# A hybrid decoder block on one core: stages that take turns where they meet, quarters staged in row slots, jobs further from their rows, another product order by rows

## Chip, cores and metric

One core of a Trainium2 chip. The metric is the device time of one execution in microseconds, the median of several runs. TensorE multiplies, VectorE and ScalarE do the element-wise work, GpSimd (POOL) issues stores and takes powers, SyncE (SP) issues loads.

## What is computed

2048 tokens of width 1024, all float32, one layer:

```python
h = rms_norm(x, norm_mix)
C, B, a, u, v, gA, gB = split(h @ w_in)              # each 1024 wide
yA = B * causal_conv3(C * a)
yB = gelu(u) * (tril(W_s[head]) @ layer_norm(gelu(v)) + b)   # within chunks of 128 tokens
x = x + (sigmoid(gA) * yA + sigmoid(gB) * yB) @ w_out
hid = relu(rms_norm(x, norm_mlp) @ w_ff1) ** 2       # 4096 wide
out = rms_norm(x + hid @ w_ff2, final_norm)
```

## The kernel before

**Products.** Tokens go in two blocks of 1024. The products of in, out, ff1 and ff2 are made by a 2x2 scheme with seven products in place of eight, named "1" to "7": of the left side sums of quarters are taken (quarter sums h11, h6, h7 and so on, kept in DRAM), of the right side `weight_sums` (L303) makes them as needed. Every factor is split into a high and a low part (`split`, L128: one copy on ScalarE, one subtraction on VectorE), and `passes` (L137) multiplies three of the four pairs of parts. So each step has four groups of three matmuls of 128x512, twelve in all, recorded at L140.

**Stages.** In order: v (32 steps) and in (168) of block 0, v and in of block 1, then out 0, out 1 (28 each), ff1 0, ff1 1, ff2 0, ff2 1 (112 each). `drive` (L290) writes the program: for step s it first emits the loads of the steps up to s + 8, then the preparations (weight sums, splits) up to s + 3, then what hangs in the step's "before" list, then the step's matmuls. TensorE and SP keep this order (L1009); ScalarE, VectorE and POOL get an order made by the scheduler, in which an instruction that is ready can stand ahead of one that the source has earlier.

**By columns** (`pair_steps`, L320; in and ff1): a pair of 128-column strips of weights is one unit of seven steps in the order "1674253"; `stagger` puts neighbouring pairs into each other, so that within a stage a pair's steps alternate with another's. Only the first and last four steps of a stage stand alone. 1, 6, 7 and 4 of a pair add on to one PSUM bank, whose state after 1, 6 and 7 ScalarE copies out.

**By rows** (`row_steps`, L663; out and ff2): "1674253" again, each product over nk row strips (4 in out, 8 in each half of ff2), on four banks. After the last strip the banks are added to the rows `x1` (L715) and 6 goes on in the bank of 1. `rows_in` (L729) loads all eight rows at once.

**Buffers.** `big` has twelve slots of 4 KB a partition for rows, `rawq` nine of 2 KB for raw weights and quarters, `half` eight of 2 KB, `wunit` four prepared weight units, `hold` seven named places for prepared left sides or weight rows; PSUM has eight banks of 128x512.

**Jobs between steps.** Norm and mix jobs of the gated branch (`ln_jobs`, L456): `norm(i)` centres and scales a row on VectorE, ScalarE and POOL (L465 to L467) and splits it; `mix(i, q)` multiplies it by the chunk weights (eight matmuls at L428), and VectorE moves the result out (L484, L485). They are spread over v from step 17 and over in from step 0. Jobs for the quarters of a later stage (`quarter_jobs`, L203): `begin` loads and norms a row, `turned` transposes it (eight matmuls at L218, two banks), `sums` adds and stores quarters. `quarters` (L259) loads one later, as four 256 KB pieces into `rawq`, and splits it into its place.

## Time and profile before

| | us |
|---|---|
| median of three runs (2704.41 to 2710.7) | 2705.53 |
| the profiled execution | 2706.06 |
| its span, first to last instruction | 2704.3 |
| TensorE busy | 2578.5 (95%) |
| VectorE busy | 1923.7 (71%) |
| ScalarE busy | 1264.5 (47%) |
| GpSimd busy | 354.2 (13%) |
| mean granted TensorE clock | 0.977 |

Busy is the time in which an engine has at least one instruction under way; matmuls are pipelined, so a busy TensorE need not be at its peak, and its counts per microsecond say more. A window is a stretch of the span with start and end in us from its beginning; an instruction that overlaps an edge is counted. "Granted clock" is the share of 2.4 GHz that TensorE was allowed; 0.5 is 1.2 GHz.

### The profile page before, as it was taken

The numbers are of one execution on the slowest core, as the hardware profiler recorded it, in microseconds if no ns is written. First come the engines' busy times: TensorE is split into PE (matmuls) and PEld (weight loads), VectorE is DVE, ScalarE is ACT, GpSimd is POOL, SyncE is SP. The second block draws the span as 40 slices with busy tenths as digits, with TensorE's granted clock in tenths as the row PEclk, the third lists the DMA queues.
The fourth block names the chain that finished last, engine by engine and source line by source line (L and its number), as shares of the span: only waits on it lengthen the run. The fifth ranks groups of instructions, "written<-read, shape, count | busy, mean of one in ns | idle before, by whom it ended". The sixth has DMA issues, their size and how long they took to land. (4 is left out here: it accounts for less than half of the span.)

```text
span 2704.3 us, 33392 instructions
## 1 busy us (share of the span) xinstructions
PE 2578.5 (95%) x11405; PEld 2125.2 (79%) x11405; DVE 1923.7 (71%) x3229; ACT 1264.5 (47%) x2205; POOL 354.2 (13%) x628
## 2 busy tenths in 40 slices
PE   8899999999899999999598999999999999999998
PEld 7778887788688888887476888778887888878886
DVE  5886776675886666778676676666657768696775
ACT  6544343344544344444235555655555444554444
POOL 1230110100330000000221222211211000000001
PEclk9999999999899999999799999999999999999999
DMA  6322433426432331354776666654448363563632
GB/s 207 91 89 67 130 112 117 139 83 198 141 94 63 90 99 54 101 205 153 259 226 210 197 191 195 206 186 158 152 145 341 118 227 108 169 251 100 223 103 78
DMA packets 297392, 410.67 MB, mean 152 GB/s; under 512 B 23509, under 2 KB 188421, under 8 KB 297221
## 3 DMA queue, kind: packets, MB, share of 16 engines
q1 hardware_dynamic: 254036, 276.91, 32.4%
q0 software_dynamic: 38576, 123.24, 13.1%
q10 hardware_dynamic: 4608, 8.39, 0.8%
q8 instruction: 89, 1.46, 0.2%
q14 instruction: 83, 0.67, 0.1%
HBM read 285.24 MB, written 123.21 MB: 151 GB/s over the span
## 5 line engine op out<-in xcount | busy, mean ns | idle before, releaser
L140 PE MATMUL ps<-hold,wu 128*128 128x512 f32 x6720 | 1546.9, 392 | 30.3 <-ACT hf L126 19.6
L140 PEld LDWEIGHTS ps<-hold,wu 128*128 128x128 f32 x6720 | 1265.9, 189 | 300.4 <-ACT hf L126 25.0
L140 PE MATMUL ps<-wu,hold 128*128 128x512 f32 x4128 | 963.6, 394 | 13.1 <-DVE big L117 7.2
L140 PEld LDWEIGHTS ps<-wu,hold 128*128 128x128 f32 x4128 | 782.8, 191 | 181.4 <-ACT wu L126 5.4
L120 DVE TENSOR_TENSOR wu<-rq,wu 128x512 fp32r<-128x512 f32 x464 | 318.9, 689 | 173.2 <-ACT wu L126 171.0
L126 ACT ACTIVATE wu<-rq 128x512 fp32r<-128x512 f32 x464 | 290.3, 627 | 301.7 <-PE ps L140 167.0
L126 ACT ACTIVATE hf<-ps 128x512 f32<-128x512 f32 x240 | 143.2, 597 | 294.3 <-PE ps L140 290.6
L120 DVE TENSOR_TENSOR wu<-hf,wu 128x512 fp32r<-128x512 f32 x240 | 165.4, 689 | 160.1 <-ACT wu L126 159.4
L126 ACT ACTIVATE wu<-hf 128x512 fp32r<-128x512 f32 x240 | 150.8, 628 | 261.2 <-DVE hf L120 128.1
L120 DVE TENSOR_TENSOR hold<-rq,hold 128x512 fp32r<-128x512 f32 x368 | 238.9, 685 | 38.8 <-ACT hold L126 38.4
L126 ACT ACTIVATE hold<-rq 128x512 fp32r<-128x512 f32 x368 | 210.8, 619 | 88.8 <-DMA rq<-h2d 30.3
L126 ACT ACTIVATE wu<-hold 128x512 fp32r<-128x512 f32 x200 | 125.3, 630 | 248.7 <-PE ps L140 234.8
L120 DVE TENSOR_TENSOR wu<-hold,wu 128x512 fp32r<-128x512 f32 x200 | 137.1, 688 | 120.9 <-ACT wu L126 120.7
L783 POOL DMA_DIRECT2D hidd<-big x224 | 122.3, 546 | 458.8 <-ACT big L771 436.7
L117 DVE TENSOR_TENSOR big<-ps,hf 128x512 f32<-128x512 f32 x120 | 82.6, 688 | 59.0 <-PE ps L140 58.7
L117 DVE TENSOR_TENSOR hf<-ps,hf 128x512 f32<-128x512 f32 x96 | 66.3, 691 | 67.1 <-PE ps L140 65.8
L117 DVE TENSOR_TENSOR big<-ps,big 128x512 f32<-128x512 f32 (+1 forms) x176 | 108.2, 670 | 7.9 <-PE ps L140 6.1
L120 DVE TENSOR_TENSOR rq<-rq,rq 128x512 f32<-128x512 f32 x160 | 110.1, 688 | 3.5 <-DMA rq<-in_w_ff_dram 0.8
L819 POOL TENSOR_TENSOR st<-st,mhalf 128x1 f32<-128x1 f32 x16 | 16.1, 1009 | 611.5 <-DVE st L818 611.5
L123 DVE TENSOR_TENSOR big<-big,hf 128x512 f32<-128x512 f32 x120 | 82.6, 688 | 11.8 <-ACT hf L600 11.7
L623 POOL DMA_DIRECT2D md<-big x56 | 30.5, 546 | 456.1 <-DVE big L117 448.9
L487 POOL DMA_DIRECT2D mixd<-hf x128 | 72.4, 566 | 101.9 <-DVE hf L484 89.3
(102 smaller groups left out, 1470.7 us busy)
## 6 DMA issues: line engine op xcount, KB each, us to landing
rq<-in_w_in_dram SPq DMA_DIRECT2D x256, 256.0 KB, 3.0
hidd<-big POOLq DMA_DIRECT2D x224, 256.0 KB, 2.8
rq<-hidd SPq DMA_DIRECT2D x224, 256.0 KB, 3.8
rq<-in_w_ff_dram SPq DMA_DIRECT2D x128, 256.0 KB, 3.2
hold<-in_w_ff_dram SPq DMA_DIRECT2D x64, 512.0 KB, 7.6
big<-x1d SPq DMA_DIRECT2D x32, 512.0 KB, 8.7
md<-big POOLq DMA_DIRECT2D x56, 256.0 KB, 4.4
rq<-md SPq DMA_DIRECT2D x56, 256.0 KB, 8.0
```

The source lines that it names most:

```text
L117: nc.vector.tensor_tensor(o, a, b, ALU.add)
L120: nc.vector.tensor_tensor(o, a, b, ALU.subtract)
L123: nc.vector.tensor_tensor(o, a, b, ALU.mult)
L126: nc.scalar.activation(o, a, AF.Copy)
L140: nc.tensor.matmul(ps, lhsT=stat_of(a), rhs=mov_of(b), start=first and n == 0, stop=last and n == 2, skip_group_check=goes_on,)
L487: nc.gpsimd.dma_start(out=mixd[blk][h + e][:, c0 : c0 + P], in_=o)
L623: nc.gpsimd.dma_start(out=md[blk][p][:, j, :], in_=src)
L783: nc.gpsimd.dma_start(out=hidd[blk][p][:, i, :], in_=src)
L819: nc.gpsimd.tensor_tensor(r, v, mhalf, ALU.pow)
```

## The change

- **Turns.** A new `weave` joins the stages: the last four steps of what is there and the first four of the next stage take turns.
- **Quarters.** `quarters` loads two pieces of 512 KB into two `big` slots; it makes four splits' work in two of double width. The first stage's quarters come three steps earlier in v of block 1; for ff1 of block 0 all seven loads stand in out 1 (steps 20 to 26), for ff1 of block 1 the first two in ff1 of block 0; the preparations stay in their steps.
- **Jobs.** A norm stands four steps before its first mix (`at_mixes`: every 3 steps in v from 17, every 2 in in from 4). A row's `begin` stands eight steps before `turned` in in, six in ff1 0, and up to six in out 1, by a list of steps.
- **Row order.** "1265734". 2, 5 and 3 take banks of their own; 6, 7 and 4 go on in those of 1. P5 is added to two quarters. Rows come in two halves, at steps 1 and 6 in out (4 and 12 in ff2); in out 1 into places 5 and 3 of `hold`, not into slots. The places of weights and left sides in the row stages are others.
- **Gate.** gelu(u) * sigmoid(gB) is gathered in two `big` slots of its own; the first four quarters are written there without a multiplication. The mixed rows (`load_mix`) come two pairs later and are multiplied in at the end, in `finish`.

```diff
+ROW_ORDER = "1265734"
+ROW_QUARTERS = {
+    "1": ((0, 0),), "2": ((0, 0),), "6": ((0, 1),), "5": ((1, 1), (0, 1)),
+    "7": ((1, 1),), "3": ((0, 1),), "4": ((1, 0),),
+}
...
         def load():
-            for r in range(CH):
-                t = rq()
-                nc.sync.dma_start(out=t, in_=src[p][:, r, :])
+            for q in range(2):
+                t = slot()
+                r = src[p][:, 2 * q : 2 * q + 2, :]
+                nc.sync.dma_start(out=t.rearrange("p (r c) -> p r c", r=2), in_=r)
                 parts.append(t)
...
             def gate(act, name, last, m, n, ps, a, j=j, st=st):
+                if name == "gate" and name not in st:
+                    st[name] = [slot() for _ in range(2)]
+                    st["fresh"] = 4
+                o = st[name][n][:, tok(m)]
+                if name == "gate" and st["fresh"]:
+                    st["fresh"] -= 1
+                    nc.scalar.activation(o, plus(o, ps, a), act)
+                    return
                 t = hf()
                 nc.scalar.activation(t, plus(t, ps, a), act)
-                o = st[name][n][:, tok(m)]
                 mul(o, o, t)
...
             def finish(j, st):
                 y1, y2 = st.pop("y")
+                for g, m, y in zip(st.pop("gate"), st["mix"], (y1, y2)):
+                    mul(g, g, m)
+                    add(y, y, g)
                 m1, m2 = st.pop("mix")
-                add(y1, y1, m1)
-                add(y2, y2, m2)
...
-                if n == 2:
+                if n == 4:
                     pr["7"]["before"].append(load_mix)
...
-            first = p in "125"
-            if first and n == 0:
-                banks[GROUP[p]] = [bank() for _ in range(CH)]
+            first = p in "1253"
+            if n == 0:
+                banks[p] = [bank() for _ in range(CH)] if first else banks["1"]
...
-                m, c = {"1": (0, 0), "6": (0, 1), "7": (1, 1)}.get(p) or QUARTER[p]
-                t = x1[r + m * CH][:, c * HB : (c + 1) * HB]
-                add(t, banks[GROUP[p]][r], t)
-                if p not in "167":
-                    finish(r + m * CH, c)
+                for m, c in ROW_QUARTERS[p]:
+                    t = x1[r + m * CH][:, c * HB : (c + 1) * HB]
+                    add(t, banks[p][r], t)
+                    if p in "2734":
+                        finish(r + m * CH, c)
...
-                ("16", "72", nxt),
+                ("14", "25", nxt),
...
-        steps[2]["before"].append(lambda: rows_in(x1, lambda i: x1d[blk][i]))
+        for m in range(2):
+            steps[(4, 12)[m]]["before"].append(
+                lambda m=m: rows_in(x1, lambda i: x1d[blk][i], m)
+            )
...
+    def at_jobs(steps, n0, every, lag, jobs):
+        begin, turned, sums = jobs
+        for n in range(2 * CH):
+            i = n // 2 + CH * (n % 2)
+            s = n0 + int(n * every)
+            at(steps, s, lambda i=i: begin(i))
+            at(steps, s + lag, lambda i=i: turned(i))
+            if n % 2:
+                at(steps, s + lag + 1, lambda r=n // 2: sums(r))
...
+    def weave(steps):
+        if phases:
+            tail, head = phases[-4:], steps[:4]
+            phases[-4:] = [f for ab in zip(tail, head) for f in ab]
+            phases.extend(steps[4:])
...
-                bring(v[22 + 3 * n], *quarters(hq, h1d[blk], p))
-            bring(inn[4], *quarters(hq, h1d[blk], "3"))
-        spread(v, 17, 0.9, 16, lambda blk=blk: late[blk, 0])
-        spread(inn, 0, 0.8, 16, lambda blk=blk: late[blk, 1])
+                bring(v[19 + 3 * n], *quarters(hq, h1d[blk], p))
+            bring(inn[5], *quarters(hq, h1d[blk], "3"))
+        at_mixes(v, 17, 3, 4, lambda blk=blk: late[blk, 0])
+        at_mixes(inn, 4, 2, 4, lambda blk=blk: late[blk, 1])
...
-            spread(inn, 44, 5, len(jobs), lambda jobs=jobs: jobs)
-        phases += v + inn
+            at_jobs(inn, 44, 11, 8, jobs)
+        weave(v)
+        weave(inn)
...
-    outs = [out_steps(blk, rotate("74253")) for blk in blocks]
+    outs = [
+        out_steps(0, "16", rotate("7425"), (None, None)),
+        out_steps(1, "74", rotate("3162162"), ("5", "3")),
+    ]
...
+            load, prep = quarters(hqs[blk], h2d[blk], p)
+            s = ff1s[blk][(0, 1, 2, 3, 4, 6, 8)[n]]
+            if blk == 0:
+                at(outs[1], min(27, 20 + n), load)
+                bring(s, nothing, prep)
...
+    for n, s in enumerate((8, 9, 10, 11, 16, 17, 18, 19)):
+        i = n // 2 + CH * (n % 2)
+        at(outs[1], (2, 3, 5, 6, 10, 11, 12, 13)[n], lambda i=i: begin(i))
+        at(outs[1], s, lambda i=i: turned(i))
+        if n % 2:
+            at(outs[1], s, lambda r=n // 2: sums(r))
+    at_jobs(ff1s[0], 16, 10, 6, h2_jobs(1))
```

## Rows read from the trace of the kernel before

**Rows 1.** The page's first part: busy time, share, instructions of each engine.

```profile
PE 2578.5 (95%) x11405; PEld 2125.2 (79%) x11405; DVE 1923.7 (71%) x3229; ACT 1264.5 (47%) x2205; POOL 354.2 (13%) x628
```

**Rows 2.** Windows, L140 alone: width, PE and PEld busy (count), clock, DMA.

```profile
1800.00:1850.00 50.00, 50.00 (x223) 41.39 (x222) 1.00 0.47 153
1850.00:1900.00 50.00, 50.00 (x222) 41.42 (x221) 1.00 0.44 141
```

**Rows 3.** The same view, end of the mixes: first L140, then L428.

```profile
765.00:795.00 30.00, 26.67 (x117) 21.43 (x116) 1.00 0.38 116
...
765.00:795.00 30.00, 4.30 (x32) 4.24 (x32) 1.00 0.38 116
```

**Rows 4.** The same view, L140 alone, four stretches.

```profile
79.00:165.00 86.00, 61.57 (x248) 47.95 (x247) 0.92 0.28 83
527.00:541.00 14.00, 10.36 (x42) 8.28 (x41) 0.88 0.74 211
676.00:795.00 119.00, 90.39 (x373) 71.26 (x372) 0.93 0.42 125
1198.00:1462.00 264.00, 204.67 (x843) 163.42 (x842) 0.90 0.68 230
```

**Rows 5.** Windows, all work: width, PE, PEld, DVE, ACT, POOL busy, clock, DMA.

```profile
79.00:165.00 86.00, 74.92 (x344) 62.02 (x343) 71.28 (x179) 39.03 (x70) 29.36 (x53) 0.92 0.28 83
...
676.00:795.00 119.00, 106.28 (x501) 88.91 (x500) 98.69 (x241) 56.40 (x102) 43.48 (x75) 0.93 0.42 125
1198.00:1462.00 264.00, 213.00 (x907) 172.44 (x906) 199.33 (x328) 106.64 (x185) 38.56 (x64) 0.90 0.68 230
1740.00:1775.00 35.00, 24.70 (x93) 18.89 (x93) 26.51 (x43) 21.84 (x41) 4.89 (x9) 0.85 0.75 236
2060.00:2100.00 40.00, 35.61 (x144) 28.60 (x144) 34.99 (x59) 18.10 (x32) 3.80 (x7) 0.91 1.00 394
2374.00:2420.00 46.00, 39.71 (x162) 30.84 (x161) 40.91 (x73) 20.74 (x39) 4.49 (x4) 0.96 0.75 278
```

**Rows 6.** Waits of PE over the span: total us, times, longest.

```profile
PE ps L218 <- DVE big L201: 40.4, 8, 24.8
...
PE ps L428 <- ACT big L126: 18.8, 6, 7.4
```

**Rows 7.** The view of rows 5, in 1 to out 0.

```profile
1198.00:1225.00 27.00, 23.57 (x101) 18.30 (x100) 25.37 (x41) 14.03 (x24) 3.81 (x7) 1.00 0.86 337
```

**Rows 8.** Timeline of DVE, end of a group in in 1.

```profile
863.14 1.23 DVE L117 TENSOR_TENSOR big<-big,big 128x1024 f32<-128x1024 f32 x1
...
874.56 1.22 DVE L117 TENSOR_TENSOR big<-big,big 128x1024 f32<-128x1024 f32 x1
875.70 0.68 DVE L120 TENSOR_TENSOR hf<-rq,hf 128x512 f32<-128x512 f32 x1
876.30 0.68 DVE L117 TENSOR_TENSOR big<-big,big 128x512 f32<-128x512 f32 x1
```

**Rows 9.** Waits of SP's queue over the span: total us, times, longest.

```profile
SPq L332 <- DVE wu L120: 1129.8, 256, 12.9
```

**Rows 10.** Timeline, out 0 to out 1: start, us, what, idle before.

```profile
1289.62 2.48 DVE L117 TENSOR_TENSOR big<-ps,big 128x512 f32<-128x512 f32 x4
1290.71 2.40 POOL L748 DMA_DIRECT2D x1d<-big  x4 [12.35 <-DVE big L117]
...
1311.83 1.06 ACT L200 ACTIVATE junk<-big 128x1024 bf16<-128x1024 f32 x1 [15.31 <-DMA big<-x1d]
...
1314.65 1.97 PE L218 MATMUL ps<-ident,big 128*128 128x128 f32 x8 [24.78 <-DVE big L201]
```

**Rows 11.** DMA issues: count, KB each, median us to landing.

```profile
big<-x1d SPq DMA_DIRECT2D x32, 512.0 KB, 8.7
...
x1d<-big POOLq DMA_DIRECT2D x16, 512.0 KB, 6.1
h2d<-hf POOLq DMA_DIRECT2D x32, 256.0 KB, 5.3
```

More of the change, by code (lines that the diff above doesn't have):

```diff
@@ L250, in sums @@
                 sink("x", a21)
-        out = []
-        for r in range(CH):
-            for i in (r, r + CH):
-                out += [lambda i=i: begin(i), lambda i=i: turned(i)]
-            out.append(lambda r=r: sums(r))
-        return out
+        return begin, turned, sums
     def quarters(hq, src, p, place=None):
@@ L270, in prep @@
             t = held(place or p)
-            for r, part in enumerate(parts):
-                tr = slice(r * P, (r + 1) * P)
-                split(t[:, 0, :, tr], t[:, 1, :, tr], part.rearrange("p (k t) -> p k t", k=CH))
+            for q, part in enumerate(parts):
+                a, b = [
+                    t[:, e, :, 2 * q * P : 2 * (q + 1) * P].rearrange("p k (r t) -> p r k t", r=2)
+                    for e in range(2)
+                ]
+                split(a, b, part.rearrange("p (r k t) -> p r k t", r=2, k=CH))
             hq[p] = t
@@ L489, in mix @@
                 st.pop(i)
-        jobs = []
-        for i in range(CH):
-            jobs += [lambda i=i: norm(i), nothing, lambda i=i: mix(i, 0), lambda i=i: mix(i, 1)]
-        return jobs
+        return norm, mix
     def v_steps(blk, hq, done):
@@ L625, in u_gate @@
             def u_gate(*a, last, j=j, st=st, gate=gate):
-                gate(AF.Gelu_apprx_tanh, "mix", last, *a)
+                gate(AF.Gelu_apprx_tanh, "gate", last, *a)
             def ga_gate(*a, last, gate=gate):
@@ L631, in gb_gate @@
             def gb_gate(*a, last, gate=gate):
-                gate(AF.Sigmoid, "mix", last, *a)
+                gate(AF.Sigmoid, "gate", last, *a)
             def with_last(f, last):
@@ L702, in run @@
                 passes(
-                    banks[GROUP[p]][r],
+                    banks[p][r],
                     lambda a: h[:, a, n % CH, r * P : (r + 1) * P],
@@ L724, in row_steps, with rows_in @@
             )
-            for p in ORDER
+            for p in ROW_ORDER
             for n in range(nk)
         ]
-    def rows_in(x1, src):
-        for i in range(2 * CH):
-            x1[i] = slot()
-            nc.sync.dma_start(out=x1[i], in_=src(i))
+    def rows_in(x1, src, m, place=None):
+        t = None if place is None else held(place, F32)
+        for i in range(CH):
+            x1[m * CH + i] = slot() if t is None else t[:, i, :]
+            nc.sync.dma_start(out=x1[m * CH + i], in_=src(m * CH + i))
     def rotate(names):
@@ L836, in ff2_steps @@
                 x1,
-                ("16", "72", nxt),
+                ("14", "25", nxt),
                 finish if chunk == 1 else lambda i, h: None,
             )
-        steps[2]["before"].append(lambda: rows_in(x1, lambda i: x1d[blk][i]))
+        for m in range(2):
+            steps[(4, 12)[m]]["before"].append(
+                lambda m=m: rows_in(x1, lambda i: x1d[blk][i], m)
+            )
         return steps
@@ L917, in at, with at_mixes @@
         steps[n]["before"].append(f)
-    def spread(steps, n0, every, count, jobs_of):
-        for i in range(count):
-            at(steps, int(n0 + i * every), lambda i=i: jobs_of()[i]())
-    phases = []
+    def at_jobs(steps, n0, every, lag, jobs):
[7 more added lines that the diff above has]
+                at(steps, s + lag + 1, lambda r=n // 2: sums(r))
+    def at_mixes(steps, n0, every, lag, jobs_of):
+        for i in range(CH):
+            at(steps, n0 + i * every, lambda i=i: jobs_of()[0](i))
+            for q in range(2):
+                at(steps, n0 + i * every + lag + q, lambda i=i, q=q: jobs_of()[1](i, q))
+    phases = []
+    def weave(steps):
[3 more added lines that the diff above has]
+            phases.extend(steps[4:])
+        else:
+            phases.extend(steps)
     for blk in blocks:
@@ L939, in hybrid_block_kernel @@
                 at(v, 15 + 3 * k, lambda k=k: first_sums(k))
-            bring(inn[0], nothing, nothing)
-            at(inn, 0, first_last)
+            at(inn, 4, first_last)
         else:
@@ L966, in hybrid_block_kernel @@
         for n, p in enumerate(ORDER):
-            bring(ff1s[blk][(0, 1, 2, 3, 4, 6, 8)[n]], *quarters(hqs[blk], h2d[blk], p))
-    jobs = h2_jobs(0)
-    spread(outs[1], 1, 0.8, len(jobs), lambda jobs=jobs: jobs)
-    jobs2 = h2_jobs(1)
-    spread(ff1s[0], 16, 4, len(jobs2), lambda: jobs2)
-    for ph in outs + ff1s + [ff2_steps(blk, rotate("453")) for blk in blocks]:
-        phases += ph
+            load, prep = quarters(hqs[blk], h2d[blk], p)
[3 more added lines that the diff above has]
+                bring(s, nothing, prep)
+            elif n < 2:
+                at(ff1s[0], 7 * NPAIR - 10 + n, load)
+                bring(s, nothing, prep)
+            else:
+                bring(s, load, prep)
+    begin, turned, sums = h2_jobs(0)
+    for n, s in enumerate((8, 9, 10, 11, 16, 17, 18, 19)):
[5 more added lines that the diff above has]
+    at_jobs(ff1s[0], 16, 10, 6, h2_jobs(1))
+    for ph in outs + ff1s + [ff2_steps(blk, nxt_g) for blk in blocks]:
+        weave(ph)
     first_norm(0)
```

18 lines of the change are left out of this document (10 added, 8 removed).

## The prediction, made before the change was run

> **What bounds it now.** I read the page first: TensorE is busy 2578.5 of 2704.3 us, far ahead of VectorE (1923.7) and ScalarE (1264.5) [rows 1]. So time comes only from stretches where TensorE does less than it can. What it can: in the middle of ff1 of block 1, with no wait, 50 us hold 222 or 223 matmuls of 128x512, one at either edge counted in both windows [rows 2]. I take 222.5, that is 0.2247 us each and 2.70 us for a step of twelve. The small matmuls: in 765 to 795 TensorE is never idle at granted clock 1.00 and does 117 large ones (26.3 us) and 32 of line 428, so these cost 3.7 / 32 = 0.116 us each [rows 3]; a mix job (8 of them) is 0.93 us. I give the transposes of line 218 the same price.
>
> Next, windows around each place where two stages meet, counting large matmuls [rows 4, 5]. What is left of the width after 0.2247 us for each large and 0.116 us for each small matmul is lost:
> - A, end of v and start of in, block 0 (79 to 165): 86 - 248 x 0.2247 - 96 x 0.116 = 19.2 us.
> - B, the same in block 1 (676 to 795): 119 - 83.8 - 128 x 0.116 = 20.4.
> - C, one transpose job in in of block 0 (527 to 541): 14 - 9.4 - 0.9 = 3.7.
> - D, out 0, out 1 and the start of ff1 0 (1198 to 1462): 264 - 189.4 - 64 x 0.116 = 67.2.
> - E, ff1 0 to ff1 1 (1740 to 1775): 35 - 20.9 = 14.1.
> - F, ff1 1 to ff2 0 (2060 to 2100): 40 - 32.4 = 7.6.
> - G, ff2 0 to ff2 1 (2374 to 2420): 46 - 36.4 = 9.6.
>
> Sum 141.8 us: what the change can reach at the most. TensorE's waits name the causes [rows 6]: 40.4 us before the transposes of line 218, for a row that is not normed yet, and 18.8 us before the mixes of line 428, for the norm in front of them. The lost time is more than the gaps, as the clock drops behind them: 0.85 to 0.96 in these windows [rows 4, 5], against 1.00 in those without a wait [rows 2, 3].
>
> Then VectorE in the same windows [rows 5]: A 71.3, B 98.7, D 199.3, E 26.5, F 35.0, G 40.9 us busy, where TensorE's own work (width less loss) is 66.8, 98.6, 196.8, 20.9, 32.4, 36.4. **In every one VectorE has as much work as TensorE or more.** So taking the waits away uncovers VectorE, and the 142 us are not to be had whole. How dense VectorE gets when it is the limit is seen at the start of out 0: 25.37 of 27 us, or 0.94, while TensorE loses time [rows 7].
>
> **The change, part by part.**
> 1. *Turns at the meetings.* The last four and first four steps of neighbouring stages alternate. It removes no instruction. It gives a step that depends on the one before it (a pair's 1, 6, 7, 4 share one bank) 2.70 us of other work in between, and spreads the entering stage's preparations over eight steps. The buffers in hold allow it by my reading of their last readers: out 0 needs place 1, and in's last reader of it is step 158 of 168.
> 2. *Lags.* A mix now stands four steps behind its norm (two before, one for the first), a transpose job eight or six behind its load (five and less). The waits of A, B and C on norms should go; the VectorE work stays.
> 3. *Another product order by rows.* 6 adds onto the bank of 1 and had to wait until VectorE had added out P1; with 2 in between it has a whole product's time. The price is four more adds a product set: P5 is added twice. In the two out stages 8 adds, whose starts are 0.60 us apart when VectorE is full [rows 8]: 4.8 us in D. In the ff2 stages 16 adds, 9.6 us, away from D; they lie beside matmuls, and cost up to 9.6 where a product 6 is already tight. I take 0.
> 4. *Quarters in row slots.* Two 1024-wide splits instead of four of 512: VectorE 2 x 1.14 against 4 x 0.60 us [rows 8], nothing. The gain is that they no longer use the nine weight buffers, for which SP waits all along (1129.8 us in 256 waits) [rows 9].
> 5. *The gate.* Four multiplies a group fewer, two 1024-wide more: -4 x 0.60 + 2 x 1.14, nothing. At a group's end one of these is added to the burst, 1.14 us. The other runs early: VectorE does not follow the source's order, the first row's add stood at 863.14, ahead of the last gate, the second at 874.56 [rows 8]. Eight groups: 0 to 9 us, covered by VectorE's idle time, 29% of the span [rows 1]; I take 0. The mixd load comes 14 steps later and still 15 ahead of its first reader: 0.
>
> **The sum.** Per stretch the floor is VectorE's work at density 0.94: A 75.8 (gain 10.2), B 105.0 (14.0), D (199.3 + 4.8) / 0.94 = 217.1 (46.9), E 28.2 (6.8), F 37.2 (2.8), G 43.5 (2.5); C loses no VectorE time, 3.7. Together 86.9.
>
> What is late next, all in D:
> - *Row 4 of block 0* is loaded at out 1's step 3, right behind out 0's last adds, and transposed at step 9. Before, the same chain (add at 1289.62, store issued 1290.71, reloaded row squared 1311.83, transposes 1314.65) took 25.0 us in a crowded moment [rows 10]; with medians (x1d 6.1, reload 8.7 [rows 11], then 2.8 us of norm by the last two stamps [rows 10], and 1.1 before the issue) 18.7. In front of it stand six steps and one transpose job, 6 x 2.70 + 0.9 = 17.1 us. Late by 1.6 to 7.9; I take 5. SP stands at that reload meanwhile, but the loads of the next eight steps are issued ahead of it, 21.6 us of work, so nothing else waits.
> - *Banks*: the transposes before step 16 need two banks, of which 1 and 5 hold all eight; two banks of 5 are free after four adds, 4 x 0.60 = 2.4 us. I take 2.5 (0 to 6).
> - *First quarters of ff1 0*: from out 1's step 19 to the first woven ff1 step are six steps, 16.2 us. Needed: two transposed halves 1.2, store 5.3, load 8.7 as for another 512 KB read [rows 11], two splits some 2.3 us. That is 17.5: 1.3 late; with a crowd 8. I take 1.5.
>
> These take 9 (2 to 22) from the gain: 87 - 9 = 78. The profiled execution took 2706.06 us (span 2704.3 and 1.8 around it), 0.5 above the median of 2705.53. 2705.5 - 78 = **2627 us**.
>
> Two rules of the Trainium skill, which the sum does without. "TensorE: Matmul & The Clock Gate", Part 1, has throttled as the default state and activity as what lifts it; so any wait that stays costs more than its length. The trace agrees: the one gap of stretch C stands beside a clock of 0.88 [rows 4], and the lost time above already holds it. "DMA: Bandwidth & Descriptors", Issuing engines are not separate DMA queues, speaks against part 4: loads put elsewhere share the same 16 DMA engines. Where stages meet they were full, share 1.00 in F and 0.75 in E and G [rows 5]; by that rule the earlier quarters slow what lands beside them, and the late items above go to their upper ends, 13 us more.
>
> **The rivals.**
> - *VectorE's work leaves the stretches.* If weaving and longer lags let it be done before and behind, where it is idle 29% of the time, TensorE alone limits them: 142 less the same 9 gives 133, so 2573 us. For it: the entering stage prepares four steps earlier. Against: D alone is 264 us long, and a step is prepared at most three ahead, with four weight buffers.
> - *Half a change.* The norms wait for row slots. Twelve slots hold, by my count at step 23 of v, three of the gating weights, five to seven rows and norm halves, four new gelu rows and perhaps a quarter: 12 to 16. If so, A and B gain nothing (24 less) and D half (23 less): 31 of 78 us are left, 2674 us. That the change doesn't do what it says is this case.
> - *Slower: SP is held by the row slots.* SP issues in one order; a quarter's load that finds no slot stops the weights behind it. The seven quarters of ff1 0 alone want 14 of 12 slots. TensorE has three prepared steps, 8.1 us; a wait beyond that stops it. SP's longest wait for buffers was 12.9 us [rows 9]. If 22 quarter loads (8 of v 1, 14 of ff1) each stood so long, each cost 4.8 us: 106 us, 2627 + 106 = 2733 us. It turns the gain into a loss from 11.7 us a load on (78 / 22 = 3.5 over 8.1). Against it: holds 1 and 6 come free before ff1 begins, so two quarters give back their slots early, and in v 1 the places are free all along.
>
> **How the numbers follow.** Forecast (2600 to 2660) 0.60; VectorE's work leaves 0.17; half a change or a bit less 0.12; no visible change 0.04; slower 0.07. What a measurement of this kernel can tell from no change is about 0.3%, 8 us. The range leaves out the slower and the unchanged case, the upper edge of half a change and the lowest of the first rival: 2570 to 2680. Faster 0.89, same 0.04, slower 0.07.
>
> **What would show it.** Right: no wait above 2 us at line 428; the 24.8 us before line 218 gone; D's counterpart some 220 us long with VectorE at 0.9 or more; F and G with no wait on the adds of line 117. Wrong: VectorE below 0.85 in D with TensorE idle (then DMA or slots are the limit), SP waits on row slots above 8 us in front of weight loads, or new idle time at the ends of groups inside in, where the gate's burst grew.

## The result, and the profile after

The changed kernel takes 2621.58 us in the median of four runs (2617.13 to 2624.03), beside 2705.95 for the kernel before on the same chip (2704.41 to 2710.7): a ratio of 0.9683, 95% interval 0.9665 to 0.9702, faster by 84.4 us. Predicted were 2627 us and 78.

The page's first part of after, to be read against [rows 1]: almost the same instructions, but less time in which TensorE has nothing under way. Its span is 2618.2 us (before 2704.3), so TensorE's idle time is 64.8 us by this line, after 125.8.

```profile
PE 2553.4 (98%) x11405; PEld 2109.8 (81%) x11405; DVE 1931.0 (74%) x3193; ACT 1258.2 (48%) x2161; POOL 351.7 (13%) x628
```

To see where the time came from I cut both traces at the same steps: twelve matmuls of 128x512 a step, counted in the order in which the steps are issued, give the start of every step. A now runs from step 16 of v to step 20 of in, B the same in block 1, D from step 160 of in 1 to step 20 of ff1 0, E from step 100 of ff1 0 to step 16 of ff1 1, F and G from step 100 of a stage to step 20 of the next. These stretches are wider than those of the prediction, so that work which was pushed to either side stays inside. First the windows of before (width, then PE, PEld, DVE, ACT, POOL busy with counts, granted clock, DMA share, GB/s): A, the middle of in 0, the step from there to B, B, D, E, F, G.

```profile
74.20:206.20 132.00, 120.92 (x562) 100.70 (x561) 113.88 (x263) 59.08 (x105) 43.83 (x78) 0.95 0.30 88
206.20:604.30 398.10, 391.54 (x1746) 322.85 (x1745) 281.70 (x429) 161.79 (x271) 42.06 (x79) 1.00 0.35 107
...
604.30:670.90 66.60, 65.56 (x290) 53.99 (x289) 37.79 (x58) 29.96 (x56) 3.79 (x7) 1.00 0.64 199
...
670.90:803.70 132.80, 120.08 (x562) 100.34 (x560) 110.79 (x260) 63.08 (x114) 44.07 (x76) 0.94 0.41 123
...
1184.50:1487.10 302.60, 251.60 (x1080) 204.48 (x1079) 223.08 (x364) 129.56 (x225) 44.37 (x74) 0.92 0.68 231
1713.80:1804.20 90.40, 80.10 (x338) 64.78 (x337) 63.81 (x101) 56.22 (x100) 15.23 (x29) 0.94 0.67 209
2032.60:2127.30 94.70, 90.31 (x385) 73.85 (x384) 77.75 (x127) 46.98 (x82) 10.80 (x20) 0.96 0.78 291
2344.90:2441.70 96.80, 90.51 (x385) 72.71 (x385) 82.12 (x144) 47.38 (x88) 8.16 (x8) 0.98 0.71 255
```

The same eight stretches of after:

```profile
73.00:195.40 122.40, 117.19 (x562) 98.30 (x561) 110.30 (x261) 57.71 (x104) 43.92 (x78) 0.97 0.30 90
195.40:598.30 402.90, 393.38 (x1744) 324.48 (x1745) 282.12 (x421) 162.81 (x272) 42.13 (x79) 0.99 0.37 111
598.30:663.60 65.30, 65.30 (x290) 54.07 (x289) 44.99 (x57) 34.95 (x57) 3.79 (x7) 1.00 0.72 235
663.60:780.00 116.40, 114.10 (x562) 96.13 (x560) 102.98 (x245) 55.92 (x99) 42.87 (x76) 1.00 0.34 104
...
1161.20:1426.60 265.40, 244.10 (x1074) 198.66 (x1073) 226.31 (x359) 126.35 (x210) 44.53 (x74) 0.97 0.75 263
...
1654.30:1732.70 78.40, 76.56 (x338) 62.92 (x337) 61.33 (x87) 54.50 (x86) 15.16 (x29) 1.00 0.72 241
1961.10:2048.20 87.10, 87.10 (x385) 72.09 (x385) 72.97 (x119) 47.14 (x82) 10.76 (x20) 1.00 0.83 312
2265.80:2355.90 90.10, 87.68 (x385) 71.92 (x384) 79.53 (x140) 47.09 (x88) 7.38 (x8) 1.00 0.73 262
```

| stretch | before | after | gain | predicted |
|---|---|---|---|---|
| A | 132.0 | 122.4 | 9.6 | 10.2 |
| middle of in 0 (holds C) | 398.1 | 402.9 | -4.8 | 3.7 |
| from there to B | 66.6 | 65.3 | 1.3 | none named |
| B | 132.8 | 116.4 | 16.4 | 14.0 |
| D (from 13 us earlier on) | 302.6 | 265.4 | 37.2 | 46.9 - 9 = 37.9 |
| E | 90.4 | 78.4 | 12.0 | 6.8 |
| F | 94.7 | 87.1 | 7.6 | 2.8 |
| G | 96.8 | 90.1 | 6.7 | 2.5 |

These add up to 86.0 of the 86.1 us between the spans; what is left, gains and losses of 1.2 us and less, cancels out. A, B and D came as forecast; E, F and G gave 26.3 in place of 12.1; inside in 0 time was lost.

TensorE's waits in after (total us, times, longest), against [rows 6]: the mixes (now line 432) wait 1.7 us at the most, and the transposes (line 223) 12.0 us in place of 40.4. New near the top are waits inside in 0 for ScalarE's copies and VectorE's sums (4.3 and 3.8 the longest).

```profile
PE ps L223 <- DVE hold L122: 12.0, 3, 7.9
PE ps L145 <- ACT hf L131: 9.9, 5, 4.3
...
PE ps L145 <- DVE big L122: 5.8, 2, 3.8
...
PE ps L432 <- ACT big L131: 1.7, 1, 1.7
```

**The longest wait left, out 1.** From the timelines of TensorE, ScalarE, VectorE and SP's queue in after (start, us, what, idle time before it and what ended it); the last line is the window behind the wait, with TensorE's granted clock third from the end:

```profile
1291.76 1.97 PE L223 MATMUL ps<-ident,big 128*128 128x128 f32 x8 [7.89 <-DVE hold L122]
1293.38 4.31 PE L145 MATMUL ps<-wu,hold 128*128 128x512 f32 x12
...
1301.94 2.98 PE L145 MATMUL ps<-wu,hold 128*128 128x512 f32 x12
...
1323.10 0.76 PE L223 MATMUL ps<-ident,big 128*128 128x128 f32 x4 [3.69 <-DVE hold L122]
...
1283.05 1.06 ACT L205 ACTIVATE junk<-big 128x1024 bf16<-128x1024 f32 x1 [4.83 <-DMA big<-x1d]
...
1284.23 0.15 DVE L198 TENSOR_SCALAR st<-st 128x1 f32<-128x1 f32 x1 [3.17 <-ACT junk L205]
...
1291.02 2.48 DVE L122 TENSOR_TENSOR hold<-ps,hold 128x512 f32<-128x512 f32 x4
...
1278.08 0.32 SPq L214 DMA_DIRECT2D big<-x1d  x1
...
1292.00:1300.00 8.00, 8.00 (x35) 6.84 (x35) 5.72 (x11) 2.27 (x5) 1.13 (x2) 0.74 1.04 398
```

Row 4 of block 0 is stored behind the last adds of out 0, and its reload is issued at 1278.08. ScalarE's next instruction in its order is the square of that row, and ScalarE stands before it for 4.83 us, till 1283.05. VectorE, which has the first small step of that row's norm next, stands 3.17 us for the square, and the adds that free the banks of product 2 come only at 1291.02, behind the scalings of two rows, though TensorE had finished product 2 at 1283.9 (1291.76 less 7.89). The transposes that wait for these banks, those of step 8, are of row 0, which had been scaled before; so the late row 4 costs time through the banks. A second wait, 3.69 us at 1323.10, stands before the transposes of step 16, for the adds of product 5. The first twelve large matmuls behind the gap take 4.31 us where twelve later ones take 2.98: at a granted clock of 0.74, between the levels of 1.2 and 2.4 GHz, 1.3 us are added.

**Behind it, the start of ff1 0.** ScalarE and TensorE in after:

```profile
1372.08 1.06 ACT L131 ACTIVATE hold<-big 128x1024 fp32r<-128x1024 f32 x1 [4.96 <-DMA big<-h2d]
...
1373.71 0.49 PE L145 MATMUL ps<-wu,hold 128*128 128x512 f32 x1 [2.69 <-ACT wu L131]
```

ScalarE stands 4.96 us before the split of a quarter of ff1 0 that has not landed. The copy of a prepared weight (1373.04) is queued behind it, and TensorE waits 2.69 us for that copy and then 0.85 for VectorE's half of the same weight.

**The same steps in E and F.** Turns change the order of steps but not their set if a stretch begins with the last four steps of a stage. So VectorE's work can be compared over the same steps near the prediction's narrow windows: from step 108 of ff1 0 to step 6 of ff1 1, and from step 108 of ff1 1 to step 10 of ff2 0, each before and then after.

```profile
1735.50:1777.00 41.50, 31.20 (x122) 24.27 (x121) 31.66 (x51) 25.50 (x47) 6.68 (x13) 0.88 0.77 242
...
1678.20:1705.50 27.30, 27.30 (x122) 22.48 (x121) 27.30 (x38) 23.55 (x36) 6.49 (x12) 1.00 0.86 290
...
2054.40:2100.10 45.70, 41.31 (x169) 33.36 (x168) 38.33 (x63) 22.69 (x40) 4.89 (x9) 0.93 1.00 396
...
1982.90:2021.00 38.10, 38.10 (x169) 31.54 (x168) 31.53 (x52) 19.37 (x35) 6.22 (x12) 1.00 0.98 379
```

In E VectorE's work in these steps falls by 4.4 us (the double splits make some of that), and what stays fills VectorE the whole time, 27.30 of 27.30 us, with TensorE as full. In F it falls by 6.8 us.

**Why in 0 grew longer.** ScalarE and GpSimd in after, from 389 us:

```profile
398.70 1.06 ACT L205 ACTIVATE junk<-big 128x1024 bf16<-128x1024 f32 x1 [3.73 <-DMA big<-in_x_dram]
...
400.27 0.57 ACT L131 ACTIVATE hf<-ps 128x512 f32<-128x512 f32 x1
...
389.24 2.96 POOL L632 DMA_DIRECT2D md<-big  x5 [5.09 <-DVE big L122]
```

The same pattern: a row for the next block's quarters is loaded at the end of a group, beside five stores of gated sums (line 632) that GpSimd issues from 389.24 on. ScalarE stands 3.73 us before its square; the copy out of PSUM of 400.27 is queued behind, then a VectorE sum, and TensorE waits 3.8 us.

### The profile page after: what moved, and what is told of

The parts are those of the page before. It is cut to its first block, busy times and chain, and to the rows that moved or that the text cites. A ratio compares the mean times of both kernels' runs of the same rounds, so it can differ in the third digit from the quotient of the medians.

```text
span 2618.2 us, 33212 instructions
## 1 busy us (share of the span) xinstructions
PE 2553.4 (98%) x11405; PEld 2109.8 (81%) x11405; DVE 1931.0 (74%) x3193; ACT 1258.2 (48%) x2161; POOL 351.7 (13%) x628
## 4 chain that ended last, share of the span: by engine, by line
PE 68%; issue 15%; DVE 6%; DMA 4%; POOL 4%; ACT 1%; SPq 0%; POOLq 0%; ACTq 0%; DVEq 0%
PE ps L145 67%; DVE wu L125 1%; POOL mixd L491 1%; DMA big<-h2d 1%; DMA big<-x1d 1%; DVE hold L125 1%; DVE big L122 1%; POOL st L200 1%; DMA big<-in_x_dram 1%; POOL hidd L797 1%; DVE hf L125 1%; POOL h2d L240 1%; DVE hf L488 0%; DVE hf L489 0%; DVE big L125 0%
## 5 line engine op out<-in xcount | busy, mean ns | idle before, releaser
L125 DVE TENSOR_TENSOR hold<-rq,hold 128x512 fp32r<-128x512 f32 x280 | 181.0, 686 | 13.8 <-ACT hold L131 13.8
L131 ACT ACTIVATE hold<-rq 128x512 fp32r<-128x512 f32 x280 | 158.9, 619 | 54.0 <-DMA rq<-md 33.9
L122 DVE TENSOR_TENSOR big<-ps,hf 128x512 f32<-128x512 f32 x144 | 99.2, 689 | 71.7 <-PE ps L145 71.6
L122 DVE TENSOR_TENSOR big<-ps,big 128x512 f32<-128x512 f32 (+1 forms) x168 | 102.9, 671 | 7.8 <-PE ps L145 6.0
L122 DVE TENSOR_TENSOR hf<-ps,hf 128x512 f32<-128x512 f32 x72 | 49.7, 691 | 49.4 <-PE ps L145 48.8
L785 ACT ACTIVATE big<-big 128x512 f32<-128x512 f32 x128 | 80.6, 629 | 2.9
```

The costliest lines, as they stand in the source:

```text
L122: nc.vector.tensor_tensor(o, a, b, ALU.add)
L125: nc.vector.tensor_tensor(o, a, b, ALU.subtract)
L131: nc.scalar.activation(o, a, AF.Copy)
L785: nc.scalar.activation(t, t, AF.Square)
```

## The experiments

The kernel before took 2703.2 to 2704.3 us beside these; a time without a spread is of one run. Stretches are cut as above. Each of the first five undoes one part. The four runs of after differ by up to 7 us, and stretches that an edit doesn't touch move too: over the kernels that leave them alone E lies between 77.0 and 80.4 us and D between 264.9 and 269.0. So of a single run less than some 4 us says nothing by itself. A stretch that comes out alike in several kernels says more.

**Turns.**

```diff
-        if phases:
+        if False:
```

> The changed kernel with its stages one behind the other again; all else stays. Theory one: the turns are what took the waits from the meetings of in to out, ff1 to ff1, ff1 to ff2 and ff2 to ff2, because they give a step that depends on the one before it other work in between and spread the preparations over twice the steps. Then the stretches from ff1 0 step 100 to ff1 1 step 16 (78.4 us in the changed kernel, 90.4 before), ff1 1 step 100 to ff2 0 step 20 (87.1, 94.7) and ff2 0 step 100 to ff2 1 step 20 (90.1, 96.8) go back by 15 us or more of the 26 together, and the ends of in lose 1 to 2 each: 2636 to 2650 us in all. Rival: row order, earlier loads and row slots did it; then the three stretches lose under 6 us together and the run is within 2620 to 2630.

Measured: 2648.28 us, so the turns are worth 26.7. Windows of this kernel for B, the end of out 1 up to step 20 of ff1 0, E and F, TensorE's longest wait in the second of these, and ScalarE's timeline in front of that wait's end:

```profile
666.30:786.60 120.30, 116.28 (x561) 97.08 (x560) 103.47 (x244) 56.17 (x99) 42.37 (x76) 0.99 0.33 99
1361.20:1446.20 85.00, 70.98 (x289) 56.44 (x288) 60.44 (x86) 43.88 (x68) 12.77 (x23) 0.90 0.63 217
1673.80:1759.70 85.90, 79.98 (x337) 64.68 (x336) 62.08 (x87) 55.03 (x86) 15.12 (x29) 0.96 0.62 203
1988.20:2077.20 89.00, 87.29 (x385) 71.99 (x384) 75.06 (x123) 47.46 (x82) 10.72 (x20) 1.00 0.83 310
...
PE ps L145 <- ACT hf L131: 12.0, 3, 10.7
...
1384.48 3.89 ACT L131 ACTIVATE hold<-big 128x1024 fp32r<-128x1024 f32 x4 [9.08 <-DMA big<-h2d]
```

The turns give 8.9 us where ff1 0 begins (85.0 against 76.1), 7.5 in E, 3.9 in B, 1.9 in F, nothing in G (89.5 against 90.1). Where a stage by columns begins alone, a pair's next product waits for ScalarE's copy of the bank that the one before it left: 0.69 us at each of the steps 2 and 3 of ff1 0, and 10.7 at step 1. These 10.7 us are not the price of a copy: ScalarE stands 9.08 us before the split of a quarter of ff1 0 that has not landed, and the copy is queued behind. With turns the same quarters cost TensorE 3.5 us (above). So where ff1 0 begins the turns mostly give late quarters time to land. Theory one holds in the total (2636 to 2650), not in the places: E, F and G together lose 8.8 us, neither the 15 of the theory nor under the 6 of its rival, and F and G hardly need turns. The Trainium skill advises interleaving regimes whose busiest engine differs ("Perfetto Trace Analysis", Optimization Strategy); no run here tests that, as TensorE has the most busy time in each of these stretches.

**Row order.**

```diff
-ROW_ORDER = "1265734"
+ROW_ORDER = "1674253"
...
-                banks[p] = [bank() for _ in range(CH)] if first else banks["1"]
+                banks[p] = [bank() for _ in range(CH)] if first else banks["5" if p == "3" else "1"]
...
```

The second add of P5 goes with it, and the first two rows of out 1 change places.

> The changed kernel with the product order 1674253 by rows as before (28 adds a product set in place of 32; 6 goes on in the bank of 1 right behind it); turns, slots, lags stay; in out 1 the first two begins change places since the lower rows are ready first. Theory one (the turns took the waits at the ff2 stages): ff1 1 to ff2 0 and ff2 0 to ff2 1 lose under 3 us each; out 0 gains a wait of 1 to 2 us at step 4 and out 1 the same, and the transposes at step 8 find four banks, those at step 16 none: 2625 to 2635 us. Rival: the order did it; PE waits again 2 to 3 us for the adds at step 8 of ff2 0 and of ff2 1, each with a lowered clock behind it, so these two stretches lose 10 us or more together: 2635 to 2645 us.

Measured: 2637.77 us, the order is worth 16.2. Windows of out 0 (steps 4 to 24) and of F with this kernel, and TensorE's waits in each:

```profile
1193.90:1260.50 66.60, 58.79 (x242) 46.71 (x241) 50.34 (x81) 20.85 (x36) 3.25 (x6) 0.95 0.42 133
1970.30:2063.80 93.50, 89.47 (x386) 73.05 (x385) 76.97 (x126) 47.14 (x82) 10.71 (x20) 0.98 0.80 295
...
PE ps L145 <- DVE big L122: 5.9, 3, 2.0
...
PE ps L145 <- DVE big L122: 4.0, 1, 4.0
```

With the old order product 6 waits again for the adds of P1 (twice in out 0, where product 7 then waits for those of P6 as well, and once in F), and out 0 takes 66.6 us against 55.0 of after, F 93.5 against 87.1, G 92.0 against 90.1; out 1 and the start of ff1 0 get 4.6 shorter. In the kernel before out 0 took 56.6 with that same order, so something in the rest of the change makes it depend on the new one; which part was not tried. The total is the rival's (2635 to 2645), but F and G lose 8.3 us together and not its 10 or more; most of the loss is in out 0, where neither theory had it.

**Quarters.** In block 1 the loads of the first stage and of ff1 go back to four pieces in weight buffers. The double splits are undone with it, and the first two loads of ff1 1, which the change has in ff1 0, go back to their steps.

```diff
+            if small:
+                for r in range(CH):
+                    t = rq()
+                    nc.sync.dma_start(out=t, in_=src[p][:, r, :])
+                    parts.append(t)
+                return
...
```

> The changed kernel with the quarters of v 1 and of ff1 1 as before: four pieces of 256 KB in the nine weight buffers, asked for with the step's loads; ff1 0 keeps the row slots. Theory one (the turns, not the row slots, shortened the meeting of the two ff1 stages; a run without turns lost 7.5 of its 12.0 us): that stretch (ff1 0 step 100 to ff1 1 step 16, 78.4 us) and v 1 (step 16 to in 1 step 20, 116.4 us) lose under 3 us each: 2621 to 2627 us. Rival (SP waits for weight buffers that hold quarters, and the weights behind come late): the ff1 stretch loses 4 us or more, 82 to 88 us, and v 1 3 or more: 2628 to 2640 us.

Measured: 2637.27 us, worth 15.7. B and E:

```profile
662.40:786.90 124.50, 115.97 (x562) 96.06 (x560) 106.67 (x254) 60.52 (x111) 43.55 (x76) 1.00 0.40 121
...
1662.70:1749.70 87.00, 80.69 (x338) 64.96 (x337) 63.59 (x101) 56.06 (x100) 15.20 (x29) 0.96 0.70 218
```

8.1 us in B and 8.6 in E are lost, as the rival had it. Which of the three did it (the buffers, the splits or, in E, the two earlier loads) is not shown. E's gain of 12.0 falls to 3.4 without this part and to 4.5 without turns: it needs both, and the two effects do not add.

**Lags.**

```diff
-        at_mixes(v, 17, 3, 4, lambda blk=blk: late[blk, 0])
-        at_mixes(inn, 4, 2, 4, lambda blk=blk: late[blk, 1])
+        for k, (norms, mixes) in enumerate((((17, 20, 24, 27), ()), ((4, 7, 10, 13), ()))):
...
+                    at((v, inn)[k], (((18, 19), (22, 22), (26, 26), (29, 30)), ((5, 6), (8, 9), (12, 12), (15, 16)))[k][i][q], lambda blk=blk, k=k, i=i, q=q: late[blk, k][1](i, q))
```

> The changed kernel with norms and mixes as close as before (norms of v at 17, 20, 24, 27, mixes one or two steps behind; in in the old list four steps later, since a mix must not stand ahead of the last row of v). Theory one (the waits of TensorE for norms were A's and B's loss): PE waits before line 432 come back, 7 us at v 1 step 18 and 2 to 4 at others; v 0 step 16 to in 0 step 20 rises from 122.3 to 127 to 134 us, block 1's from 116.4 to 125 to 133: 2635 to 2650 us. Rival (VectorE's amount of work or the turns alone set these stretches): under 4 us each.

Measured: 2648.40 us, worth 26.8. A, and the waits before the mixes:

```profile
73.60:208.90 135.30, 121.47 (x562) 101.14 (x561) 113.78 (x262) 58.44 (x105) 43.26 (x78) 0.95 0.28 83
...
PE ps L432 <- ACT big L131: 14.3, 5, 3.8
```

A is 12.9 us longer and B 10.8 (127.2), as theory one had it: without the lag the whole of A's gain is gone and two thirds of B's, and the waits before the mixes are back (14.3 us here, 1.7 in after).

**Gate.** The old gate, with its four multiplications, mixd load and short end.

```diff
-                for g, m, y in zip(st.pop("gate"), st["mix"], (y1, y2)):
-                    mul(g, g, m)
-                    add(y, y, g)
+                add(y1, y1, m1)
+                add(y2, y2, m2)
...
```

> The changed kernel with the old gate: the gates are multiplied into the mixed rows as they come, these are loaded in the third pair again (at its fourth step), no rows of its own for the gate. Asked: in of block 0, steps 20 to 160, takes 402.9 us in the changed kernel and 398.1 before, though the one wait for transposes is gone. Theory one: the new finish (one 1024-wide multiplication more at the end of each group) does it; then that stretch falls to 398 or below, and block 1's (381.2 against 380.8) by a little. Rival: the row jobs do it, which now fall on the ends of groups; a row's load stands beside seven stores and ScalarE's queue stands at its square; then the stretch stays at 401 to 404 us.

Measured: 2622.27 us, no difference in all. The middle of in 0 takes 399.3 us instead of 402.9, that of in 1, which has no row jobs, 381.6 instead of 381.2. What in 0 gains is lost again in stretches that the edit doesn't touch (1.6 to 2.1 us each in D, ff1 0 and E). So the gate alone costs nothing (in 1), and its burst at a group's end costs where a row job meets it.

**Row jobs away from the ends of groups.** On after; the eight row loads of in 0 come in two lots of four, each lot between two ends of groups (steps 44, 86 and 128).

```diff
-            at_jobs(inn, 44, 11, 8, jobs)
+            for n, s in enumerate((50, 58, 64, 72, 92, 100, 106, 114)):
+                i = n // 2 + CH * (n % 2)
+                at(inn, s, lambda i=i, begin=begin: begin(i))
+                at(inn, s + 8, lambda i=i, turned=turned: turned(i))
...
```

> The changed kernel with the row jobs of in 0 moved between the ends of groups (steps 44, 86, 128): begins at 50, 58, 64, 72, 92, 100, 106, 114, transposes eight steps behind each as now; nothing else. Theory one (the new finish makes in 0 longer): in 0's steps 20 to 160 stay at 400 us or more, the run within 0.1% of the changed kernel. Rival (the jobs fall on the ends of groups: a row is asked for at step 88, right behind the seven stores of step 86, lands 7.5 us later, and ScalarE's queue stands 3.7 us at its square; sums at 130 stand behind the finish of 128): the waits of 3.8 and 4.3 us at steps 93 and 132 go with their lowered clock, the stretch falls to 390 to 396 us, and the run to 2608 to 2615 us, faster than both kernels.

Measured: 2615.82 us (2614.01 to 2618.36), ratio 0.968 [0.9664, 0.9697]. The middle of in 0 with the old gate, and then with the jobs between:

```profile
194.70:594.00 399.30, 392.40 (x1745) 324.15 (x1746) 283.75 (x431) 163.04 (x272) 42.08 (x79) 0.99 0.36 111
```

```profile
195.50:591.90 396.40, 390.18 (x1745) 321.56 (x1746) 280.20 (x421) 163.13 (x272) 43.49 (x79) 1.00 0.38 113
...
PE ps L145 <- ACT hf L131: 6.2, 5, 1.6
```

The two waits of 3.8 and 4.3 us are gone, the longest for a copy is 1.6, and the stretch is 6.5 us shorter: the -4.8 was the meeting of row jobs and group ends, as the rival had it. The stretch repeats: 395.7 to 396.7 us in the four kernels with the jobs between, 401.8 to 404.2 in the eight with the new gate and the jobs at their old steps. The whole kernel can't be told from after by the ratios to the kernel before (0.968 and 0.9683).

**Out 1's wait.** Three kernels. The first, on after, norms the rows of x in place of those of the sum, so that nothing waits for the store of out 0's rows; it leaves the product of out 0 out of ff1 0 and so computes something else:

```diff
-    begin, turned, sums = h2_jobs(0)
+    begin, turned, sums = quarter_jobs(lambda i: x[i * P : (i + 1) * P, :], G_MLP, h2d[0])
```

> The changed kernel with the quarters of ff1 block 0 made of rows of the input in place of rows of out 0 (the residual sum is left out there), so that no reload waits for the store of a row. Theory one (row 4 of block 0 is late: its reload waits 8.6 us in SP's queue for the store, ScalarE's and VectorE's queues stand at its square and norm, and the adds of product 2, whose banks the first transposes need, come behind them): the wait of 7.9 us before the transposes at out 1 step 8 falls under 3 us, out 0 step 24 to out 1 step 24 (101.7 us) falls by 5 to 9 us: 2612 to 2617 us. Rival (VectorE's amount of work is the limit there, full from 1284 to 1294): the transposes wait 6 us or more still, the stretch changes by under 3 us.

Measured: 2622.75 us; the wait shrinks from 7.9 to 5.3 and out 1 by 2.0 us, and the start of ff1 0 takes 3.5 more. Waiting for the store is a third of the wait; the rest is what stands ahead of the adds in VectorE's order. The rival is nearer, with a stretch changed by under 3 us.

The second, on the kernel with jobs between, loads the first half of out 1's own rows in out 0:

```diff
+    outs, first_half = [o[0] for o in outs], outs[1][1]
+    at(outs[0], 18, first_half)
...
```

> The run with the jobs between the ends of groups, and the first four input rows of out 1 asked for in out 0 at step 18 in place of out 1's step 1, when the DMA engines are half idle. Theory one (the stores and reloads of out 0's rows are slow because 2 MB of weights, 2 MB of input rows and 2 MB of stores meet there; stores land 10 to 15 us after their issue): stores of rows 0 to 3 land in 6 to 9 us, the first transposes of out 1 wait 4 us or less: 2608 to 2613 us. Rival (the wait is for VectorE's order, or for the rows whose adds come last): the transposes wait 6 us or more still and the run is within 2 us of the run with the jobs between the ends alone (2615.8).

Measured: 2615.82 us (2614.72 to 2618.48), ratio 0.9674 [0.9655, 0.9692], no difference to the kernel with jobs between, with a longest wait of 6.8 in place of 8.2, as the rival had it.

The third, also on jobs between, puts most of the transposes of out 1 a step later:

```diff
-    for n, s in enumerate((8, 9, 10, 11, 16, 17, 18, 19)):
+    for n, s in enumerate((9, 10, 11, 11, 17, 18, 19, 19)):
```

> The run with the jobs between the ends of groups, and the transposes of out 1 one or two steps later: 9, 10, 11, 11 and 17, 18, 19, 19 in place of 8 to 11 and 16 to 19, so that they no longer stand right behind product 2 and 5, whose adds must free their banks. Theory one (a matter of order: the adds come behind other work in VectorE's queue, and one step between would hide them): the waits of 7.9 and 3.7 us before transposes fall to 2 or less together, out 1 steps 4 to 24 (77.8 us) falls by 5 us or more: 2607 to 2612 us. Rival (the amount: VectorE has no room in out 1, the wait only moves to the steps behind): the stretch and the run change by under 2 us, and TensorE waits for weight units or adds instead.

Measured: 2611.44 us (2608.64 to 2614.74), ratio 0.966 [0.9644, 0.9676]. TensorE's waits in out 1 with this kernel, where after has the 12.0 us shown above:

```profile
PE ps L223 <- DVE hold L122: 6.9, 3, 5.5
PE ps L145 <- ACT wu L131: 3.6, 1, 3.6
```

A step of 2.7 us takes 5.1 us off the waits before the transposes, and 3.6 come back as a wait for a prepared weight. Out 1 from step 4 to step 24 is only 0.7 us shorter than with the jobs between alone (77.1 against 77.8), not 5: theory one fell, and the wait mostly moved. Of the 4.4 us between the medians most lies in the start of ff1 0 (73.5 against 76.0) and in E (77.2 against 79.5); why is not shown.

**Where G came from.** Two kernels. On after, all rows of ff2 at step 2, as before:

```diff
-            steps[(4, 12)[m]]["before"].append(
+            steps[(2, 2)[m]]["before"].append(
```

> The changed kernel with all eight rows of a ff2 stage asked for at its step 2 as before, not in halves at steps 4 and 12. Asked: ff2 0 to ff2 1 (step 100 to step 20) fell by 6.7 us, of which the run without turns gave back none and the old product order 1.9. Theory one (the rows in halves: at step 2 SP stands at the four or more rows for which the twelve slots have no room until the old block's last rows are stored, 9.5 us before, and the weights behind come late): that stretch goes back by 3 to 7 us, 93 to 97 us; ff1 1 to ff2 0 by 0 to 2: 2624 to 2631 us. Rival (it is the other places of weights and left sides, in which a weight row finds its place free earlier): under 1.5 us in either stretch, 2619 to 2624 us.

Measured: 2617.55 us, G 87.7 instead of 90.1 (eight kernels with the halves have 90.1, alike to 0.1 us). The halves cost 2.4 us there; theory one was the wrong way round. On the kernel without turns, places for left sides that begin anew in each ff2 stage:

```diff
-    for ph in outs + ff1s + [ff2_steps(blk, nxt_g) for blk in blocks]:
+    for ph in outs + ff1s + [ff2_steps(blk, rotate("673")) for blk in blocks]:
```

> The stages follow each other without turns, as in the kernel without turns (2648.3 us), and each of the two ff2 stages begins its own round of places 6, 7, 3 for left sides, as the kernel before did with 4, 5, 3. A stage's last half product is the 28th, so it lies in the first place of the round, and the next stage's first strip wants that same place. Theory one: this is where the ff2 0 to ff2 1 stretch got its 6.7 us from, as the split of the first strips must now wait for the last matmul of the stage before: the stretch goes from 89.5 us back to 94 to 97, with a TensorE wait for the copy into a left side at the start of ff2 1, as the 1.0 us one in the kernel before. Rival: the places don't matter, the gain came from the other product order and from buffers freed elsewhere; 89 to 91 us and no such wait.

Measured: 2642.9 us, and G:

```profile
2290.20:2378.50 88.30, 87.58 (x385) 71.89 (x384) 77.35 (x137) 47.32 (x88) 7.00 (x8) 1.00 0.74 272
```

88.3 us with no wait there, not 94 to 97: theory one fell. Of G's 6.7 us the row order made 1.9; turns, rows in halves and the round of left-side places made none of it. Untried are the places of the weight rows and parts taken away together, so its source stays open.

**The best parts together.** The later transposes with all ff2 rows at step 2.

> The kernel with jobs between group ends and the transposes of out 1 one step later (2611.4 us), with the rows of ff2 loaded all at step 2 and not in halves at 4 and 12. Theory one: the 2.4 us that this gave in the ff2 0 to ff2 1 stretch come on top: 87.7 us there, 2609 us in all, the fastest. Rival: one earlier reading was an accident of the schedule, or the eight rows take slots which the other changes use: 90 us there and 2611 to 2613 in all.

Measured: 2609.18 us (2606.26 to 2613.66), ratio 0.9649 [0.9636, 0.9662].

G takes 87.9 us: the 2.2 us are there again (90.1 without), but the start of ff1 0, which has not been edited, takes 76.4 us against 73.5. In all this kernel and the one with later transposes can't be told apart. They lie 12 and 10 us below after; by the intervals of the ratios only the 12 are clear of it.

## Why the prediction was right, step by step

The total was 5 us off; larger errors cancelled out, so that much of the agreement is luck. Two of its sums are off in the last digit, without weight for the forecast: A loses 19.1 us and not 19.2, and the load that would turn the gain into a loss is 11.6 us and not 11.7.

- *A, B and D by VectorE's work at 0.94: right in size, not in mechanism.* 9.6, 16.4 and 37.2 against 10.2, 14.0 and 37.9. The limit itself was not reached: VectorE is busy 0.90 of A, 0.88 of B and, over the wider D, 226.31 of 265.4 us, 0.85 and not "0.9 or more", and TensorE still loses 31 us there (265.4 - 1010 x 0.2247 - 64 x 0.116). In A and B VectorE's work did not stay, as part 2 had it: 113.88 us became 110.30 in A and 110.79 became 102.98 in B, and in the stretch ahead of B 37.79 became 44.99. That is how B beat its floor. In D the sum had 20.3 us for VectorE's floor (217.1 less TensorE's 196.8) and 9 for what is late; the run shows a VectorE that is not full and more that is late (below).
- *E, F, G: the failed step.* The floor there was VectorE's work at density 0.94 in windows of 35 to 46 us, as if none of it could leave them and none of it could be denser. Over the same steps VectorE's work fell by 4.4 us in E, 6.8 in F and 2.6 in G (49.36 to 46.77, from step 108 to step 13), and its density was 1.00 in E and 0.95 in G. The first rival's mechanism, with a chance of 0.17, was right for these three: 26.3 of the 31.3 us lost there came back, not 12.1. F shows no gap at all.
- *C: wrong sign.* 3.7 us were to come and 4.8 were lost. The wait that the term priced did go: before line 218 there were 2.4 us of waits in this stretch, before line 223 there are none. The missed term is the meeting of row jobs with the ends of groups, for which part 5 had its bounds (0 to 9 us for the burst, taken as 0), and "new idle time at the ends of groups inside in" was named as a sign of being wrong. The burst alone costs nothing (in 1); beside a row job it costs time, as the runs with the old gate (3.6 us back) and with the jobs between (6.5 back) show.
- *What is late next: the right items, undersized.* They were taken as 9 us (2 to 22) and came to some 15.5 of TensorE's waits. Row 4 (5): 7.9 us, by the banks of product 2 and not before row 4's own transposes, as ScalarE and VectorE work off their queues in order. Banks before step 16 (2.5): 3.7 and 0.4. First quarters of ff1 0 (1.5): 2.7 and 0.85, by ScalarE's queue and a prepared weight, and 10.7 without turns.
- *The row order: right in F, mis-sized elsewhere.* It was to remove the wait of 6 for the adds of P1; without it F is 6.4 us longer. That out 0 would need it (11.6 us) could not be read from the trace of before, where out 0 took 56.6. D's VectorE work grew by 3.2 us (223.08 to 226.31) with all parts together, for 4.8 forecast.
- *Quarters.* "Nothing" for VectorE was nearly so: E has 61.33 us of its work with the change and 63.59 with this part undone. The part is worth 15.7 us, and the prediction had put no number to it.
- *Rivals that fell.* Half a change: A and B gained in full. SP held by row slots: its longest wait for a row slot, at line 743, is 8.2 us, just over the bound of 8, and the longer ones at loads of quarters and rows (9.2 and 8.6) are for stores of the data itself (the quarters of ff1 0 are the late item above); in B and E, for which quarters are loaded, TensorE is idle for 2.3 and 1.8 us in all. The price of this rival was read too low: before, SP's waits at line 332 reached 15.9 us, not 12.9, which was the longest of one of their causes.
- *Shares.* The parts undone one by one lose 26.7 + 16.2 + 15.7 + 26.8 = 85.4 us, the whole gained 84.4. As E and out 0 show, that this fits is not proof that they add.
- *The rule on DMA engines* (the Trainium skill, "DMA: Bandwidth & Descriptors", Issuing engines are not separate DMA queues) was to cost up to 13 us more. The late items took half of that, 6.5 us more than the 9, at a share that rose in D from 0.68 to 0.75; no run shows how much of it is contention, and D as a whole came out within 0.7 us of its forecast. *The rule on the clock* (the Trainium skill, "TensorE: Matmul & The Clock Gate", Part 1) agrees: 1.3 us of slow matmuls behind the gap of 7.89.

## What to carry to other kernels

Put the load of a row or a quarter, its norm or split and its first reader apart by more than the slowest landing, and away from bursts of stores: an instruction that waits for a late load holds up all that stands behind it on ScalarE and VectorE, and TensorE's wait then bears the name of something else (a bank, a prepared weight). So look at what stands in front of the releaser on its own engine. Take the limit of a busy second engine over the window into which its work can move, not over the stretch in which TensorE waits, and don't take a density seen in one stretch (0.94) as a cap: E ran at 1.00. Undo the parts one by one, and look at every stretch: a part can carry a stretch (out 0 here) that was not in trouble before.

## What was not expected of the hardware

For 24 us around the meeting of out 0 and out 1 the sixteen DMA engines were full, and TensorE worked on: this window of after has a DMA share of 1.00 at 379 GB/s with TensorE busy 21.92 of 23.90 us at granted clock 1.00. The one gap, of 2.02 us at its end, is for adds of VectorE and not for a load. That full engines cost nothing is not shown by it: the eight stores of out 0's rows, issued from 1251.0 to 1274.9, took 5.0 to 15.0 us to land (median 8.7), and the late row 4 waited for one of them.

```profile
1248.80:1272.70 23.90, 21.92 (x97) 17.83 (x95) 19.72 (x33) 9.02 (x16) 2.14 (x4) 1.00 1.00 379
```
